# Forming the Strassen right operands in place and on VectorE, three single-pair chunk pairs at either end, and weight roundings on ScalarE

## The chip, the cores and the metric

The kernel runs on one core of a Trainium2 chip. The metric is the time of one execution in device microseconds (us), as the median of three runs. The page and the rows come from one further execution that the hardware profiler recorded. PE is TensorE, DVE is VectorE, ACT is ScalarE, POOL is GpSimd; SP issues nearly all DMAs.

## The reference

One encoder layer runs over two requests (16 meta tokens and 256 prompt tokens; 16 meta tokens and 1024 sample tokens) with shared float32 weights:

```python
h = concat([meta, x])
h = h + 0.5 * swiglu(rmsnorm(h, norm_ffn1), ffn1_w_gate, ffn1_w_up, ffn1_w_down)
u = rmsnorm(h, norm_mix) @ w_in
o = diff_attention(q, k, v, lam, bias)      # 4 heads, two softmax maps each
p = pool_mixer(p_in, pool_w, pool_scale)    # windows 2, 4, 8, 16
h = h + concat([rmsnorm(o) * 0.8, p]) @ w_out
h = h + 0.5 * swiglu(rmsnorm(h, norm_ffn2), ffn2_w_gate, ffn2_w_up, ffn2_w_down)
y = rmsnorm(h, norm_final)[:, 16:]
# swiglu(x, g, u, d) = (silu(x @ g) * (x @ u)) @ d ; D_MODEL 1024, D_FF 2816
```

## The kernel before

Activations stand transposed: features on the 128 partitions (8 k-tiles `c`), tokens along the row, 1296 tokens in FFN1 (the two requests' shared meta tokens doubled), 1280 in FFN2. A float32 matmul is done as three matmuls of rounded parts (`mm3`, L157 to L159): high weight by high input, low by high, high by low. Forming a part therefore takes two steps: a rounding ("hi") and a subtraction of it ("lo"). For weights POOL makes the hi (L145) and DVE the lo (L148); for inputs ACT makes the hi (L142).

**Gate and up projections.** Each FFN splits its tokens into four blocks (324 or 320 tokens) that go in two pairs, (0,2) and (1,3). For each of 11 chunk pairs `j` of 256 output features, `gate_up` calls `seven` once for the gate weight and once for the up weight. `seven` computes a 2x2 block product (two halves of the features of the input by two blocks of tokens, two output chunks) by seven products in place of eight, in the order b11, t1, t2, b22, t3, b21, t4. A product is 4 k-tiles by 3 matmuls for each pair in `subs`; a `seven` is 84 matmuls on one pair and 168 on both. Its left operands come from `s_parts`: four raw quarter blocks, and four sums of them that DVE forms (L359, L362, L367, L374). It has three raw buffers of 512 KB (`wraw`), and five of the parts' buffers (RING). Results are kept by ACT (L399) and added by DVE (L409, L413, L417); up's results go to memory (L439) and are read again as `hraw` by the down projection, where ACT rounds them and DVE or POOL makes the lo.

**Right operands T.** For a token pair, `t_tasks` makes b11, b22, b21, t1 to t4: DVE multiplies by gain and by the row of inverse norms (L322) into an `xf` buffer, POOL makes four subtractions, ACT the hi and DVE the lo, k-tile pair `c` by pair (`c` 0 to 3). All seven products need all four `c`. Pair 0's T is formed from `h` while tokens of the second group come in (`token_in`, `token_rows`); then `h` goes to `h1_d`, and pair 1's T is formed from there, as tasks that `pump()` starts after each k-tile of a product.

**Order of chunk pairs.** Chunk pair 0 runs for pair 0 alone while T[1] is formed ("first single set"); chunk pairs 1 to 10 run on both pairs; chunk pair 0 runs for pair 1 alone ("second single set"), after which the freed memory takes `h` again (three whole loads, L634) for the down projection. FFN2 does the same; its `h` comes out of the w_out projection (L1182), which also runs pair by pair with the same (0,2), (1,3), forms T[0] when the first pair is done, and adds up squares for the norms (L1145, L1154).

Within an engine the order is what the tile scheduler chose; a DMA waits on SP for its operands with the DMAs behind it.

Of the kernel before, what the change touches and what calls it, by code (L numbers as in the profile page):

```python
# [19 lines left out]
P = 128  # L20
# [17 lines left out]
PAIRS = ((0, 2), (1, 3))  # L38
# [60 lines left out]
def encoder(ctx: ExitStack, tc: tile.TileContext, a: dict):  # L99
# [207 lines left out]
    def t_tasks(key, T, n, get, gain, rows, xp):  # L307
# [3 lines left out]
        def load(c):  # L311
            for cc in (c, c + 4):
                for side in range(2):
                    x[cc, side] = get(cc, side)

        def norm(c):
            for cc in (c, c + 4):
                for side in range(2):
                    src, dst = x[cc, side]
                    if dst is None:  # L320
                        dst = xp.tile([P, NS], F32, tag="xf", name="xf", bufs=5)[:, :n]
                    nc.vector.scalar_tensor_tensor(  # L322
                        out=dst, in0=src, scalar=gain[:, cc : cc + 1], in1=rows[side], op0=ALU.mult, op1=ALU.mult
                    )
                    x[cc, side] = dst

        def sums(c):
            b11, b12, b21, b22 = (x.pop((cc, side)) for cc in (c, c + 4) for side in range(2))
            split(c, b11=b11, b22=b22, b21=b21)
# [16 lines left out]
        return out

    def s_parts(w, j, tp):

        r0, r1 = raw_cols(w, 2 * j), raw_cols(w, 2 * j + 1)  # L350
# [14 lines left out]
        hi_pool(h2, f2)  # L365
# [4 lines left out]
        hi_pool(h4, f4)  # L370
# [52 lines left out]
    def gate_up(j, T, blocks, subs, wg, wu, hid, tp, bufs):  # L423

        n = blocks[0][1]
# [9 lines left out]
        def up(s, fi, ti, c, in_psum=False):  # L435
            o = g[s, fi, ti] if in_psum else c
            nc.vector.tensor_mul(o, g[s, fi, ti], c)
            t0 = blocks[PAIRS[s][ti]][0]
            nc.sync.dma_start(out=hid[2 * j + fi][:, t0 : t0 + n], in_=o)  # L439

        seven(wg, j, T, n, subs, tp, temp, gate)
# [4 lines left out]
    def down_tasks(h, blocks, hid, wd, hp):  # L446
        order = list(range(1, NF // 2)) + [0]
# [89 lines left out]
    def token_in(i, tok, h, ss):  # L537

        t0, m = TOK[i]
        for half in range(2):  # L540
# [5 lines left out]
            (nc.vector.tensor_copy if half else nc.scalar.copy)(out=h[:, 4 * half : 4 * half + 4, t0 : t0 + m], in_=psv)  # L546
        nc.scalar.activation(out=tok, in_=tok, func=AF.Square, accum_out=ss[:m])
# [45 lines left out]
    tasks.extend(
        t_tasks(
            ("t", 0),
            T[0],
            NS,
            lambda c, side: (h[:, c, part_of(PAIRS[0][side])], None),
            gains["norm_ffn1"],
            [row[:, part_of(b)] for b in PAIRS[0]],  # L600
            xp,
        )
    )
# [4 lines left out]
    token_rows(TOK_ORDER[1], ss[1], row)
    for lo, hi in ((0, 384), (384, 640), (640, 1024), (1024, T1)):
        nc.sync.dma_start(out=h1_d[:, :, lo:hi], in_=h[:, :, lo:hi])  # L610
    pump(len(tasks))
# [12 lines left out]
    for j in range(1, NF // 2):  # L624
        gate_up(j, T, BS1, (0, 1), wg, wu, hid1_d, tp, 18)
# [6 lines left out]
    first, down = down_tasks(h, BL1, hid1_d, a["ffn1_w_down"][0], hp)  # L632
    for b, (s, n) in enumerate(BL1):
# [698 lines left out]
```

## Time and profile before

| | |
|---|---|
| median of 3 runs | 2537.6 us (2537.16 to 2540.35) |
| the profiled execution | 2537.2 us, span 2535.4 us |
| mean granted PE clock | 0.959 of full |
| busy PE, DVE, ACT, POOL | 2354.2, 1484.1, 597.5, 675.7 us |
| PE's share of the chain that ended last | 81% |

A busy PE is not a PE at its peak: its matmuls take longer when the granted clock is low, and the gaps between them are small. The stages along the time are FFN1 to about 650 us with its down projection behind, w_in and the attention up to 1469, w_out to 1617, FFN2's gate and up to 2205, down projection and last norm to the end.

### The profile page before, as it was taken

To read this page: it belongs to the slowest core of one execution; us is meant where nothing else is said; L and a number is where in the kernel's file an instruction comes from. 1 tells how busy PE (TensorE), PEld (TensorE's weight loads), DVE (VectorE), ACT (ScalarE), POOL (GpSimd) and SP (SyncE) were. 2 spreads that over 40 slices of the span, in tenths; PEclk is the share of its full clock that TensorE was granted. 3 is DMA by queue.
4 is the path that set the end of the run, shared out by engine and by line. 5 is a ranking of instruction groups with operands and counts; after the bars stand their busy time and mean duration, and the time that the engine had idled before them with its cause. 6 is when DMAs were issued, how large, how long until landed. Compare 5 with 4: busy or idle time off the path is not lost.

```text
span 2535.4 us, 38469 instructions
## 1 busy us (share of the span) xinstructions
PE 2354.2 (93%) x14578; PEld 2202.0 (87%) x14578; DVE 1484.1 (59%) x2726; ACT 597.5 (24%) x1341; POOL 675.7 (27%) x879
## 2 busy tenths in 40 slices
PE   3799999999999998999878887799999999999998
PEld 3699999999888887899778887689999999888886
DVE  6844544544767766344477737575444454666765
ACT  5321111111111113111467623221111111111113
POOL 3411111111212124111377635331111111211112
PEclk6899999999999999999999998789999999999999
DMA  6312221224422323645644154322212222622322
GB/s 206 90 55 74 73 71 57 78 76 147 132 76 85 96 71 113 174 147 165 165 132 122 48 155 127 104 78 77 77 55 76 72 70 64 222 83 77 98 71 84
DMA packets 270386, 256.30 MB, mean 101 GB/s; under 512 B 20369, under 2 KB 229865, under 8 KB 269689
## 3 DMA queue, kind: packets, MB, share of 16 engines
q1 hardware_dynamic: 270200, 253.85, 32.8%
q8 instruction: 115, 1.88, 0.3%
q14 instruction: 71, 0.57, 0.1%
HBM read 182.40 MB, written 75.61 MB: 102 GB/s over the span
## 4 chain that ended last, share of the span: by engine, by line
PE 81%; DVE 5%; POOL 4%; DMA 4%; issue 2%; ACT 2%; SPq 1%; POOLq 0%; ACTq 0%; DVEq 0%
PE bank L157 26%; PE bank L158 26%; PE bank L159 26%; DMA v<-v_d 1%; DVE xf L322 1%; DVE wl L148 1%; POOL l L831 1%; PE bank L848 1%; PE pair L800 1%; PE pair L801 1%; DMA hc<-h_d 1%; POOL xf L330 1%; DMA hraw<-hid_d 1%; PE bank L237 1%; SPq L783 0%
## 5 line engine op out<-in xcount | busy, mean ns | idle before, releaser
L145 POOL TENSOR_SCALAR wh<-wraw 128x512 fp32r<-128x512 f32 x296 | 213.2, 723 | 788.0 <-PE bank L159 490.4
L148 DVE TENSOR_TENSOR wl<-wraw,wh 128x512 fp32r<-128x512 f32 x296 | 226.6, 769 | 329.4 <-POOL wh L145 328.8
L479 DVE SCALAR_TENSOR_TENSOR h<-bank,h 128x272 f32<-128x272 f32 (+2 forms) x528 | 312.7, 601 | 151.3 <-PE bank L159 147.1
L157 PE MATMUL bank<-hl,wh 128*128 128x512 f32 (+2 forms) x1056 | 380.1, 360 | 0.0
L158 PE MATMUL bank<-hl,wl 128*128 128x512 f32 (+2 forms) x1056 | 379.4, 359 | 0.0
L159 PE MATMUL bank<-hl,wh 128*128 128x512 f32 (+2 forms) x1056 | 378.8, 359 | 0.0
L399 ACT COPY hid<-bank 128x324 f32<-128x324 f32 (+1 forms) x264 | 112.9, 428 | 659.5 <-PE bank L159 650.5
L145 POOL TENSOR_SCALAR wh<-ws 128x512 fp32r<-128x512 f32 x192 | 126.2, 660 | 526.7 <-PE bank L159 327.0
L159 PEld LDWEIGHTS bank<-hl,wh 128*128 128x128 f32 x1056 | 199.1, 189 | 31.8
L157 PEld LDWEIGHTS bank<-hl,wh 128*128 128x128 f32 x1056 | 199.1, 189 | 31.7
L158 PEld LDWEIGHTS bank<-hl,wl 128*128 128x128 f32 x1056 | 198.9, 188 | 31.5
L148 DVE TENSOR_TENSOR wl<-ws,wh 128x512 fp32r<-128x512 f32 x192 | 142.2, 744 | 99.5 <-POOL wh L145 99.5
L142 ACT CAST hl<-hraw 128x272 fp32r<-128x272 f32 (+2 forms) x132 | 72.5, 552 | 519.3 <-PE bank L158 395.2
L157 PE MATMUL bank<-t2h,wh 128*128 128x324 f32 (+1 forms) x352 | 112.1, 318 | 13.0 <-POOL wh L145 13.0
L157 PE MATMUL bank<-t1h,wh 128*128 128x324 f32 (+1 forms) x352 | 110.9, 316 | 7.0 <-POOL wh L145 7.0
L157 PE MATMUL bank<-b22h,wh 128*128 128x324 f32 (+1 forms) x352 | 110.7, 314 | 7.2 <-POOL wh L145 5.0
L158 PE MATMUL bank<-t4h,wl 128*128 128x324 f32 (+1 forms) x352 | 110.1, 313 | 6.5 <-DVE wl L148 6.5
L158 PE MATMUL bank<-t2h,wl 128*128 128x324 f32 (+1 forms) x352 | 111.6, 317 | 4.6 <-DVE wl L148 4.6
L157 PE MATMUL bank<-t3h,wh 128*128 128x324 f32 (+1 forms) x352 | 110.1, 313 | 4.7 <-POOL wh L145 4.7
L157 PE MATMUL bank<-t4h,wh 128*128 128x324 f32 (+1 forms) x352 | 110.0, 312 | 3.5 <-DVE hid L413 3.5
L158 PE MATMUL bank<-t1h,wl 128*128 128x324 f32 (+1 forms) x352 | 111.7, 317 | 1.2 <-DVE wl L148 0.7
L158 PE MATMUL bank<-t3h,wl 128*128 128x324 f32 (+1 forms) x352 | 110.3, 313 | 1.6 <-DVE wl L148 1.6
(217 smaller groups left out, 6293.8 us busy)
## 6 DMA issues: line engine op xcount, KB each, us to landing
wraw<-in_ffn_w_gate SPq DMA_DIRECT2D x48, 512.0 KB
wraw<-in_ffn_w_up SPq DMA_DIRECT2D x48, 512.0 KB
hraw<-hid_d SPq DMA_DIRECT2D x88, 256.0 KB
wraw<-in_ffn_w_down SPq DMA_DIRECT2D x44, 512.0 KB
hid_d<-hid SPq DMA_DIRECT2D x88, 162.0 KB
hid_d<-hid SPq DMA_DIRECT2D x88, 160.0 KB
k<-k_d SPq DMA_DIRECT2D x32, 260.0 KB
h<-h_d SPq DMA_DIRECT2D x4, 2048.0 KB
```

The lines of the kernel that those rows point to most:

```text
L142: nc.scalar.copy(out=out, in_=in_)
L145: nc.gpsimd.tensor_scalar(out=out, in0=in_, scalar1=1.0, scalar2=1.0, op0=ALU.mult, op1=ALU.mult)
L148: nc.vector.tensor_sub(out, in_, hi.bitcast(F32))
L157: nc.tensor.matmul(out=ps, lhsT=wh, rhs=xh, start=first, stop=False, skip_group_check=on)
L158: nc.tensor.matmul(out=ps, lhsT=wl, rhs=xh, start=False, stop=False, skip_group_check=on)
L159: nc.tensor.matmul(out=ps, lhsT=wh, rhs=xl, start=False, stop=last, skip_group_check=on)
L237: nc.tensor.matmul(out=ps[:, j * m : (j + 1) * m], lhsT=r[:, j : j + 1].broadcast_to([m, P]), rhs=ident[:m, :m], start=True, stop=True,)
L322: nc.vector.scalar_tensor_tensor(out=dst, in0=src, scalar=gain[:, cc : cc + 1], in1=rows[side], op0=ALU.mult, op1=ALU.mult)
L330: nc.gpsimd.tensor_sub(b11, b12, b11)
L399: nc.scalar.copy(out=to[s], in_=ps[s])
L479: nc.vector.scalar_tensor_tensor(out=h[b][:, m], in0=ps, scalar=0.5, in1=h[b][:, m], op0=ALU.mult, op1=ALU.add)
L800: nc.tensor.matmul(out=ps[:, m], lhsT=qs, rhs=kh[:, ks], start=True, stop=False)
```

## The change

- Pair 0's T is formed **in place** in `h`, in product order: fourteen steps (`t_in_place`), each of two k-tiles; all sums are on DVE, and lo's are 128x648. Since `h` is overwritten, each token tile goes to `h1_d` right after it came in (eleven writes in place of four), and the norm waits for these. The first two raw weights are loaded ahead of it.
- Pair 1's T (`t_loaded`) has its loads, norms, lo's, sums and lo's as separate tasks with gaps between them; sums on DVE.
- Chunk pairs 0, 1, 2 run for pair 0 alone, 3 to 10 for both, 0, 1, 2 for pair 1 alone, in both FFNs (`SINGLE1`, `SINGLE2`). Weight parts of a chunk pair that runs alone are loaded and formed twice.
- The hi of weight parts in `s_parts` is on ACT; of the other weights it stays on POOL.
- `h` for the down projection is loaded in 12 pieces, one for each seven calls of `pump`.
- FFN2's pairs are (0,1), (2,3). `cat` has a tile for each block and channel; four channels of block 1 are loaded during the attention. `hc` loads run two ahead. T[0] is formed in place under w_out's second pair; gate_up starts when it is done, and the second pair's norm rows are made inside gate_up.

```diff
-PAIRS = ((0, 2), (1, 3))
+PAIRS1 = ((0, 2), (1, 3))
+PAIRS2 = ((0, 1), (2, 3))
+SINGLE1 = 3
+SINGLE2 = 3
...
-    def parts_of(raw):
+    def parts_of(raw, hi_of=hi_pool):
...
-        hi_pool(wh, raw)
+        hi_of(wh, raw)
...
+    def t_split(T, c, k, **f):
+        for name, v in f.items():
+            th, tl = (t[:, c : c + k] for t in T[name])
+            hi_act(th, v)
+            lo_dve(tl, v, th)
+
+    def spread(key, fs, gap):
+        return [(key, g) for f in fs for g in [f] + [None] * gap]
...
+        def t1(c):
+            x = X(c, 0)
+            nc.vector.tensor_sub(x, norm(c, 1), x)
+            t_split(T, c, 2, t1=x)
...
+        return [lambda f=f, c=c: f(c) for f in (b11, t1, t2, b22, t3, b21, t4) for c in (0, 2)]
...
-            nc.gpsimd.tensor_sub(b11, b12, b11)
-            nc.gpsimd.tensor_sub(b12, b22, b12)
-            nc.gpsimd.tensor_sub(b22, b22, b11)
-            nc.gpsimd.tensor_sub(b21, b21, b22)
...
+            nc.vector.tensor_sub(b11, b12, b11)
+            nc.vector.tensor_sub(b12, b22, b12)
+            nc.vector.tensor_sub(b22, b22, b11)
+            nc.vector.tensor_sub(b21, b21, b22)
...
-        hi_pool(h1, f1)
+        hi_act(h1, f1)
...
+        nc.sync.dma_start(out=h1_d[:, :, t0 : t0 + m], in_=h[:, :, t0 : t0 + m])
         nc.scalar.activation(out=tok, in_=tok, func=AF.Square, accum_out=ss[:m])
...
+    tasks.extend(spread(("t", 1), [None, lambda: token_rows(TOK_ORDER[1], ss[1], row), None], 4))
+    tasks.extend(spread(("t", 1), t_loaded(T[1], NS, h1_d, places[1], gains["norm_ffn1"], rows[1], xp), 5))
+    for j in range(SINGLE1):
+        gate_up(j, T, places, NS, (0,), wg, wu, hid1_d, tp, 9, raws if j == 0 else None)
...
-    for b, (s, n) in enumerate(BL1):
-        nc.sync.dma_start(out=h[b], in_=h1_d[:, :, s : s + n])
-    first = first()
-    gate_up(0, T, BS1, (1,), wg, wu, hid1_d, tp, 10)
...
+    tasks.extend(spread(("h", 0), load_h(h, h1_d, BL1), 6))
+    for j in range(SINGLE1):
+        if j == SINGLE1 - 1:
+            parts0 = first()
+        gate_up(j, T, places, NS, (1,), wg, wu, hid1_d, tp, 10)
...
-                        hc = tx.tile([P, NS], F32, tag="hc", name="hc", bufs=2)[:, :n]
-                        nc.sync.dma_start(out=hc, in_=h_d[:, m, s : s + n])
...
+                        hc = got[b, m]
...
-    ensure(("row", PAIRS[1][1]))
-    pump(len(tasks))
+    ensure(("t", 0))
```

The next two fences are DVE at the start of FFN1, first of before and then of after: T[0] being formed beside the token tiles of the second group (`h` copies from a `bank`); b11l to t4l are the lo parts of T, `xf` and `h` their unrounded values.

```order
L148 TENSOR_TENSOR t2l<-xf,t2h 128x324
L148 TENSOR_TENSOR t4l<-xf,t4h 128x324
L322 SCALAR_TENSOR_TENSOR xf<-h,g_norm_ffn_208,row 128x324 x4
L546 COPY h<-bank 128x4x128
L148 TENSOR_TENSOR b11l<-xf,b11h 128x324
L148 TENSOR_TENSOR b22l<-xf,b22h 128x324
L148 TENSOR_TENSOR b21l<-xf,b21h 128x324
```

```order
L152 TENSOR_TENSOR t1l<-h,t1h 128x648
L589 COPY h<-bank 128x4x128
L338 TENSOR_TENSOR h<-h 128x2x324
L328 SCALAR_TENSOR_TENSOR h<-h,g_norm_ffn_208,row 128x324
L589 COPY h<-bank 128x4x128
L343 TENSOR_TENSOR h<-h 128x2x324
L152 TENSOR_TENSOR t1l<-h,t1h 128x648
```

Before, the last lo of one k-tile (t4l) stands ahead of the first of the next (b11l), so no product is whole until all is; after, one operand follows another, whole, and the subtractions stand among them on DVE.

The next two are SP where the both-pair chunk pairs of FFN1 end and the second single set begins, before and after: `h` is the residual, `hraw` the hidden values for the down projection, `wraw` the raw weights.

```order
L634 DMA h_5864<-h_d 128x8x272
L439 DMA hid_d_104<-hid 128x324 x2
L634 DMA h_5865<-h_d 128x8x512
L634 DMA h_5866<-h_d 128x8x512
L454 DMA hraw<-hid_d_85 128x272
L454 DMA hraw<-hid_d_86 128x272
L454 DMA hraw<-hid_d_85 128x512
L164 DMA wraw<-in_ffn_w_up 128x8x128
```

```order
L670 DMA h_5411<-h_d 128x2x512
L670 DMA h_5409<-h_d 128x2x272
L670 DMA h_5410<-h_d 128x2x512
L168 DMA wraw<-in_ffn_w_up 128x8x128
L168 DMA wraw<-in_ffn_w_gate 128x8x128
L670 DMA h_5411<-h_d 128x2x512
L670 DMA h_5409<-h_d 128x2x272
L670 DMA h_5410<-h_d 128x2x512
L670 DMA h_5411<-h_d 128x2x512
L505 DMA hraw<-hid_d_89 128x272
```

Eight of the twelve pieces of `h` still stand ahead of up's second raw weight, but no `hraw` does.

The last two are ACT in the both-pair chunk pairs (gate, then up), before and after: COPY L399 and L451 keep a product's sum, `wh` is the hi of a weight part.

```order
L399 COPY hid_2944<-bank_2918 128x324 [waits DMAHW2_49,PE_49]
L399 COPY hid_2946<-bank_2931 128x324 [waits DMAHW3_49,PE_49]
L399 COPY hid_2984<-bank_2958 128x324 [waits DMAHW4_49,PE_49]
L399 COPY hid_2986<-bank_2971 128x324 [waits DMAHW5_49,PE_49]
L399 COPY hid_3018<-bank_2918 128x324 [waits DVE_49,PE_49,Activation_49]
```

```order
L451 COPY hid_3261<-bank_3235 128x324 [waits DMAHW7_49,PE_49]
L451 COPY hid_3263<-bank_3248 128x324 [waits DMAHW0_49,PE_49]
L146 CAST wh_3403<-wraw_3189 128x512 [waits DMAHW5_49,Activation_49]
L451 COPY hid_3295<-bank_3195 128x324 [waits PE_49]
L451 COPY hid_3297<-bank_3208 128x324 [waits PE_49]
L146 CAST wh_3439<-wraw_3435 128x512 [waits DMAHW6_49,Activation_49]
```

Weight roundings now stand behind copies that wait for PE.

## Rows read from the trace of the kernel before

**Rows 1.** Windows: length, busy (x count) of PE, PEld, DVE, ACT, POOL, PEclk, DMA share, GB/s.

```profile
0.00:20.00 20.00, 9.25 (x53) 8.81 (x54) 5.15 (x15) 10.82 (x19) 2.03 (x7) 0.94 0.92 311
80.00:100.00 20.00, 8.13 (x36) 7.14 (x36) 17.85 (x31) 9.21 (x21) 10.46 (x10) 0.74 0.27 83
120.00:600.00 480.00, 480.00 (x3234) 480.00 (x3233) 231.79 (x401) 87.43 (x197) 84.02 (x135) 1.00 0.22 70
...
1620.00:1640.00 20.00, 9.04 (x32) 7.57 (x30) 16.68 (x27) 7.60 (x19) 10.35 (x11) 0.50 0.14 41
...
1680.00:2160.00 480.00, 480.00 (x3273) 480.00 (x3272) 235.45 (x407) 87.78 (x199) 86.99 (x138) 1.00 0.22 70
```

**Rows 2.** Timeline of PE: start, length, idle before and what ended it.

```profile
61.67 0.64 PE L157 MATMUL bank<-b11h,wh 128*128 128x324 f32 x1
...
112.36 0.31 PE L157 MATMUL bank<-b11h,wh 128*128 128x324 f32 x1
...
611.42 0.31 PE L157 MATMUL bank<-b11h,wh 128*128 128x324 f32 x1
...
650.09 0.29 PE L157 MATMUL bank<-hl,wh 128*128 128x272 f32 x1
...
1477.55 0.64 PE L157 MATMUL bank<-ch,wh 128*128 128x320 f32 x1 [8.23 <-ACT ch L142]
...
1573.62 0.64 PE L158 MATMUL bank<-ch,wl 128*128 128x320 f32 x1 [11.07 <-DVE wl L148]
...
1616.19 1.23 PE L1154 MATMUL bank<-ones,acc 128*80 128x1 f32 x8 [5.51 <-DVE acc L1145]
1617.27 0.61 PE L157 MATMUL bank<-b11h,wh 128*128 128x320 f32 x1
...
1676.34 0.31 PE L157 MATMUL bank<-b11h,wh 128*128 128x320 f32 x1
...
2169.45 0.31 PE L157 MATMUL bank<-b11h,wh 128*128 128x320 f32 x1
...
2205.34 0.28 PE L157 MATMUL bank<-hl,wh 128*128 128x256 f32 x1
```

**Rows 3.** Timeline of DVE while T[0] and the first weight parts are formed.

```profile
21.28 0.56 DVE L322 SCALAR_TENSOR_TENSOR xf<-h,g_norm_ffn,row 128x324 f32<-128x324 f32 x1 [2.44 <-ACT row L562]
...
34.16 1.17 DVE L148 TENSOR_TENSOR b21l<-xf,b21h 128x324 fp32r<-128x324 f32 x1
...
40.02 0.49 DVE L148 TENSOR_TENSOR b11l<-xf,b11h 128x324 fp32r<-128x324 f32 x1
40.42 0.49 DVE L148 TENSOR_TENSOR b21l<-xf,b21h 128x324 fp32r<-128x324 f32 x1
...
58.93 0.68 DVE L148 TENSOR_TENSOR wl<-ws,wh 128x512 fp32r<-128x512 f32 x1
59.53 0.68 DVE L367 TENSOR_TENSOR ws<-wraw,ws 128x512 f32<-128x512 f32 x1
```

**Rows 4.** The page's groups: busy us and mean ns of one, then idle time before.

```profile
L145 POOL TENSOR_SCALAR wh<-wraw 128x512 fp32r<-128x512 f32 x296 | 213.2, 723 | 788.0 <-PE bank L159 490.4
L148 DVE TENSOR_TENSOR wl<-wraw,wh 128x512 fp32r<-128x512 f32 x296 | 226.6, 769 | 329.4 <-POOL wh L145 328.8
...
L399 ACT COPY hid<-bank 128x324 f32<-128x324 f32 (+1 forms) x264 | 112.9, 428 | 659.5 <-PE bank L159 650.5
...
L142 ACT CAST hl<-hraw 128x272 fp32r<-128x272 f32 (+2 forms) x132 | 72.5, 552 | 519.3 <-PE bank L158 395.2
```

**Rows 5.** Timeline of SP, and of DVE, in FFN1's second single set.

```profile
624.53 0.38 SPq L164 DMA_DIRECT2D wraw<-in_ffn_w_up  x1
...
634.09 0.68 DVE L359 TENSOR_TENSOR ws<-wraw 128x512 f32<-128x512 f32 x1
```

More of the change, by code (lines that the diff above doesn't have):

```diff
@@ L305, in t_tiles, with t_in_place, norm, b11 @@
         return {k: tuple(pool_.tile([P, 4, n], F32R, tag=f"{k}{t}", name=f"{k}{t}", bufs=1) for t in "hl") for k in T_NAMES}
-    def t_tasks(key, T, n, get, gain, rows, xp):
+    def t_split(T, c, k, **f):
[5 more added lines that the diff above has]
+        return [(key, g) for f in fs for g in [f] + [None] * gap]
+    def t_in_place(T, X, gain, rows):
+        def norm(c, side):
+            x = X(c, side)
+            for i in range(2):
+                nc.vector.scalar_tensor_tensor(
+                    out=x[:, i], in0=x[:, i], scalar=gain[:, c + i : c + i + 1], in1=rows[side], op0=ALU.mult, op1=ALU.mult
+                )
+            return x
+        def b11(c):
+            t_split(T, c, 2, b11=norm(c, 0))
+        def t1(c):
+            x = X(c, 0)
+            nc.vector.tensor_sub(x, norm(c, 1), x)
+            t_split(T, c, 2, t1=x)
+        def t2(c):
+            x = X(c, 0)
+            nc.vector.tensor_sub(x, norm(c + 4, 1), x)
+            t_split(T, c, 2, t2=x)
+        def b22(c):
+            t_split(T, c, 2, b22=X(c + 4, 1))
+        def t3(c):
+            x = X(c, 1)
+            nc.vector.tensor_sub(x, X(c + 4, 1), x)
+            t_split(T, c, 2, t3=x)
+        def b21(c):
+            t_split(T, c, 2, b21=norm(c + 4, 0))
+        def t4(c):
+            x = X(c + 4, 0)
+            nc.vector.tensor_sub(x, x, X(c, 0))
+            t_split(T, c, 2, t4=x)
+        return [lambda f=f, c=c: f(c) for f in (b11, t1, t2, b22, t3, b21, t4) for c in (0, 2)]
+    def t_loaded(T, n, src, starts, gain, rows, xp):
         x = {}
@@ L437, in up, with down_tasks @@
             nc.vector.tensor_mul(o, g[s, fi, ti], c)
-            t0 = blocks[PAIRS[s][ti]][0]
+            t0 = places[s][ti]
             nc.sync.dma_start(out=hid[2 * j + fi][:, t0 : t0 + n], in_=o)
-        seven(wg, j, T, n, subs, tp, temp, gate)
+        seven(wg, j, T, n, subs, tp, temp, gate, raws)
         seven(wu, j, T, n, subs, tp, temp, up)
-    def down_tasks(h, blocks, hid, wd, hp):
-        order = list(range(1, NF // 2)) + [0]
+    def down_tasks(h, blocks, hid, wd, hp, single):
+        order = list(range(single, NF // 2)) + list(range(single))
         def prep(g):
@@ L583, in encoder @@
         nc.vector.memset(t, 1.0)
-    def part_of(b):
-        return slice(BS1[b][0], BS1[b][0] + NS)
+    places = [[BS1[b][0] for b in pair] for pair in PAIRS1]
+    rows = [[row[:, s : s + NS] for s in pair] for pair in places]
     toks = [token_dma(i, hp) for i in TOK_ORDER[0]]
     load_gain("norm_ffn1")
+    raws = raw_cols(wg, 0), raw_cols(wg, 1)
     for j, i in enumerate(TOK_ORDER[0]):
@@ L592, in encoder @@
     token_rows(TOK_ORDER[0], ss[0], row)
[L593 to L603, printed above, removed]
+    steps_ = t_in_place(T[0], lambda c, side: h[:, c : c + 2, places[0][side] : places[0][side] + NS], gains["norm_ffn1"], rows[0])
+    for f in steps_[:2]:
+        f()
     for j, i in enumerate(TOK_ORDER[1]):
-        pump(2)
         token_in(i, token_dma(i, hp), h, ss[1][:, j : j + 1])
-    pump(len(tasks))
[L608 to L611, printed above, removed]
+        for f in steps_[2 + 3 * j : 5 + 3 * j]:
+            f()
     gst.close()
@@ L623, in encoder @@
     bst_, tp = scope("tmpb", side="right")
-    for j in range(1, NF // 2):
-        gate_up(j, T, BS1, (0, 1), wg, wu, hid1_d, tp, 18)
+    for j in range(SINGLE1, NF // 2):
+        gate_up(j, T, places, NS, (0, 1), wg, wu, hid1_d, tp, 18)
     bst_.close()
@@ L1162, in encoder @@
     raws = [raw_cols(w_out, m) for m in range(2)]
-    for b in PAIRS[0]:
+    places = [[BS2[b][0] for b in pair] for pair in PAIRS2]
+    for b in PAIRS2[0]:
         s = BS2[b][0]
@@ L1166, in encoder, with load_hc @@
         nc.sync.dma_start(out=h[b], in_=h_d[:, :, s : s + n])
-    for i, pair in enumerate(PAIRS):
-        for b in pair:
-            if b:
-                for c in order:
-                    cat_part(b, c, tx, 4)
+    for b in range(3):
+        for c in CAT_ORDER:
+            if (b, c) not in cat:
+                cat_part(b, c, tx, 3)
+    ahead = [(b, m) for m0 in range(0, KC, 2) for b in PAIRS2[1] for m in (m0, m0 + 1)]
+    got = {}
+    def load_hc():
+        if ahead:
+            b, m = ahead.pop(0)
+            got[b, m] = tx.tile([P, NS], F32, tag="hc", name="hc", bufs=3)[:, :n]
+            nc.sync.dma_start(out=got[b, m], in_=h_d[:, m, BS2[b][0] : BS2[b][0] + n])
+    for i, pair in enumerate(PAIRS2):
+        if i:
+            load_hc()
+            load_hc()
+            for c in CAT_ORDER:
+                cat_part(pair[1], c, tx, 3)
         for m0 in range(0, KC, 2):
```

142 lines of the change are left out of this document (70 added, 72 removed).

## The prediction, made before the changed kernel ran

> **What bounds the kernel now.** I read the windows first [rows 1], for the granted clock and PE's share by stage, then PE's timeline at the stages' edges [rows 2], then what DVE does there [rows 3, 5], and took durations from the page's groups and from spacings [rows 3, 4]. In the both-pair stages of the two FFNs PE is full: 3234 matmuls in 480 us at clock 1.00 (0.1484 us each), 3273 in FFN2 (0.1467) [rows 1]. There DVE is busy 232 of 480 us and ACT 87: no other engine is near its end. What is not full are four places beside these: the first single set of each FFN, w_out, and the second single sets. In them PE waits for DVE or for a weight part, and the clock falls to 0.50 to 0.74 [rows 1]; at 0.50 (1.2 GHz) 32 matmuls took 9.04 us, 0.28 each. A single set is 168 matmuls: 24.9 us (FFN1), 24.6 us (FFN2) at full clock. Measured [rows 2]:
>
> - FFN1's first product starts at 61.67; the set ends at 112.36.
> - Its second set, 611.42 to 650.09, takes 38.7, 13.7 too many.
> - w_out: PE begins to wait at 1469.3 (1477.55 less 8.23) and starts FFN2 at 1617.27, 148.0. The loops issue 768 matmuls, of which 48 had run; 720 are worth 105.6; 42.4 too many.
> - FFN2's first set, to 1676.34, takes 59.1, 34.4 too many.
> - Its second set, 2169.45 to 2205.34, takes 35.9, 11.2 too many.
>
> FFN2 thus loses 88.0 us around its edges, FFN1 13.7 and its slow start. The change goes at these.
>
> **FFN1's start.** DVE sets it. Undisturbed, a 128x324 takes 0.41 us from one to the next, a 128x512 0.60 [rows 3]. Before, DVE can start normalizing at 21.28 [rows 3], but T is whole only at 61. After, the norm also waits until the first group's six `h1_d` writes (3.1 MB) landed. The nearest row is the first window: 311 GB/s with the engines 92% busy [rows 1]; at that rate 3.1 MB last 10 us, most of it beside the copies that feed it, so I take 24. From there the changed order gives DVE, for T[0], 16 norms at 0.45, 8 subtractions and 14 lo's of two k-tiles at 0.82, and five copies at 0.6: 28 us. T[1] is 60 instructions at 0.41, 24.6. A `seven` needs 11 weight instructions at 0.60 and 3 (gate) or 7 (up) on 128x324: 7.8 or 9.5. By the order DVE stands at the end of T[1] when it has done the weights of four and a half sevens, some of those ahead of 24: 86 us of work, to 110. Ten products (120 matmuls, 17.8) are then left to PE: 128 without any wait. For waits on token tiles, the round trip through ACT and stretches at half clock I add 2 to 9 and take 133. Six sevens are over then. Before, two were over at 112.36 and four more would be worth 49.9, to 162.3. **Gain 29 (25 to 35).** T[1]'s own cost is nothing only while the three sets' 74.8 us of PE cover it; DVE has 52 + 24.6 us in the same span, so the cover is thin and the set goes at DVE's pace, which the sum has in it.
>
> The extra forming costs loads too: eight more sevens' weights, 8 MB, in a kernel that moves 70 GB/s in these stages [rows 1]: hidden.
>
> **FFN1's second sets.** Before, up's second raw weight was issued at 624.53 behind `h` and `hraw`, and DVE began its first sum at 634.09 [rows 5]. After, `hraw` comes only ahead of the third set, when 50 us of singles have passed; but eight of the twelve `h` pieces still stand ahead of that weight, and gate's first sum still stands on DVE behind the last results of the both-pair stage. I leave one such restart: 4 (1 to 8) in place of 13.7. **Gain 10 (6 to 13).**
>
> **FFN2's start.** Five losses take the place of 88.0.
> - The wait for `cat` (8.23) stays, since the `h` loads still stand ahead of it: 8, and 1.5 for the clock after it.
> - Under w_out's second pair, T[0], with the weights' and sums' own work between, is 26 us of DVE by the same count beside 28 of PE. The 11.07 us for one `wl` [rows 2] came from a whole T standing ahead of it on DVE; now weight lo's stand between the steps. One still stands behind the eighth sum: 6 (2 to 12).
> - The 5.51 for `acc` [rows 2] goes, but the second pair's norm columns now stand on DVE ahead of gate's first sum, behind the last projection: 7.
> - The three single sets: DVE has 53.8 us up to the last T[1] lo (counted from the changed order, at the same spacings), against 44 of PE by then; with restarts 14 (9 to 20).
> - The second sets, as in FFN1: 3 (1 to 7).
>
> Sum 39.5, **gain 48 (36 to 58)**.
>
> **Hi on ACT.** In a both-pair `seven` ACT gets seven roundings more. Its rows are 0.43 for a 128x324 copy and 0.55 for a rounding of mixed shapes [rows 4], so some 4 us in 24.9, on an engine that was busy 87 of 480 us. Its queue is in order, and roundings stand behind copies that wait for PE. With five buffers a part is due four products after its buffer comes free, 14 us; copy, rounding and lo are 1.6. I take zero, and price the contrary below. DVE gains by POOL's silence: beside POOL's subtractions a b21 lo took 1.17, alone 0.49 [rows 3], and the mean `wl` was 0.77 [rows 4]. The sum already goes by undisturbed spacings. The Trainium skill, GPSIMD Engine Reference, section Specifications, says that POOL shares its SBUF interfaces with DVE and contends with DVE instructions that have two SBUF inputs; these rows agree. Had POOL stayed busy, six sevens would have 42 `wl` at 0.77 in place of 0.60, 7 us more for each first set.
>
> **The attention** keeps its order but for three more `cat` loads: 0, within 5 either way. The sum: 29 + 10 + 48 = 87. The profiled execution took 2537.2 (span 2535.4 and 1.8 around it), beside a median of 2537.6. 2537.2 less 87 is 2450.
>
> **The rivals.**
>
> *The single sets are bound elsewhere.* Twelve sevens run alone in each FFN; each needs two raw loads through three buffers, ACT, DVE and PE in turn within 12.5 us. If restarts and the half clock cost 1.5 to 3 us more in each of 24, the gain falls by 36 to 72: 2486 to 2515. For: every single set now loses 11 to 34 us, and one fall to 0.50 makes 84 matmuls take 23.5 us. Against: these sets formed T or loaded `h` and `hraw` within two sevens, and six now share that.
>
> *The writes hold the start.* Eleven `h1_d` writes of 128-token rows stand on SP ahead of the second group's tokens, and the norm waits for six of them. If they move at half the 311 GB/s, the start is 10 us later: 2460. The DMA share of 0.92 in that window [rows 1] speaks for it; that the second window's tokens come in while DVE has T to form speaks against. The Trainium skill, DMA: Bandwidth & Descriptors, section Measured, gives 341 GB/s for 1 MB and 138 for 64 KB and asks for 1 MiB transfers; the change cuts `h1_d` and `h` the other way. By its lower figure, an estimate, the six writes would last 23 us and the time be 2462; the row's 311 was reached with pieces of 512 KB, so I hold the upper end likelier.
>
> *More comes back.* If the singles are not bound by DVE but keep PE full, FFN2's start loses 22 rather than 39.5 and FFN1 starts 6 earlier: 2427.
>
> *ACT's queue holds the both-pair stages (slower).* 32 both-pair sevens now get their hi from ACT. If the copies of a product and the roundings behind them lock step, each of three such roundings delays its part by rounding and lo, 1.15: 3.5 us in each, 110 in all, 2560. It decides from 2.7 us a `seven` (87/32). Against it stand the four products of lead.
>
> *It does not do what it says.* If the scheduler puts the in-place steps behind the waits that they were to avoid (h1_d writes after all tokens, the last `acc`), the start and FFN2's edge stay and only the eased loads of the second sets remain, 10, paid by the extra forming: 2537 within 5.
>
> **How the numbers follow.** Forecast 2450 with its own range 2430 to 2478 (the ends of its three gains, not all at once; the writes' rival lies in it): 0.64. Singles bound elsewhere, 2478 to 2515: 0.20. More comes back, below 2430: 0.06. No change: 0.04. Slower: 0.06. To hold 8 in 10, the range takes the forecast's own, the better half of the first rival and a little below: 2428 to 2492. Faster by over 0.2% (5 us, about what a measurement of this kernel can tell from no change): 0.64 + 0.20 + 0.06 = 0.90; within: 0.04; slower: 0.06.
>
> **What would show it.** FFN1's first products near 30 us and its third single set over near 133; both-pair stages still at 1.00 without PE waits, at 24.9 and 24.6 us a `seven`; the second sets' six sevens near 79 us; no 11 us wait for `wl` in w_out; FFN2's first product 10 to 15 us after the last projection's matmuls at most, and three sets in 88. Wrong would be: PE waiting for `wh` by ACT in the both-pair stages, a clock at 0.50 through a single set, a first norm after 30, or singles waiting for raw loads.

## The result and the profile after

| | before | after |
|---|---|---|
| median | 2537.4 us (4 runs, 2534.7 to 2540.35) | 2452.1 us (4 runs, 2450.31 to 2457.24) |
| ratio | | 0.9667, 95% interval 0.9649 to 0.9685 |
| the profiled execution, its span | 2537.2, 2535.4 | 2450.3, 2448.5 |
| mean granted clock | 0.959 | 0.979 |
| busy PE, DVE, ACT, POOL | 2354, 1484, 598, 676 | 2336, 1506, 804, 388 |

PE's timeline of the changed kernel at the same edges as [rows 2]: start, length, and the idle time before with what ended it.

```profile
34.70 0.42 PE L161 MATMUL bank<-b11h,wh 128*128 128x324 f32 x1
...
134.47 0.31 PE L161 MATMUL bank<-b11h,wh 128*128 128x324 f32 x1
...
533.69 0.31 PE L161 MATMUL bank<-b11h,wh 128*128 128x324 f32 x1
...
612.34 0.28 PE L161 MATMUL bank<-hl,wh 128*128 128x272 f32 x1
...
1520.83 0.63 PE L162 MATMUL bank<-ch,wl 128*128 128x320 f32 x1 [6.11 <-DVE wl L152]
...
1549.95 0.31 PE L163 MATMUL bank<-cl,wh 128*128 128x320 f32 x1
1550.10 0.31 PE L161 MATMUL bank<-b11h,wh 128*128 128x320 f32 x1
...
1556.88 0.63 PE L161 MATMUL bank<-t1h,wh 128*128 128x320 f32 x1 [3.78 <-ACT wh L146]
...
1646.34 0.31 PE L161 MATMUL bank<-b11h,wh 128*128 128x320 f32 x1
...
2040.82 0.31 PE L161 MATMUL bank<-b11h,wh 128*128 128x320 f32 x1
...
2118.36 0.28 PE L161 MATMUL bank<-hl,wh 128*128 128x256 f32 x1
```

The first single set of FFN1 ends at 134.47, the second runs from 533.69 to 612.34; FFN2's first product is at 1550.10, its sets run to 1646.34 and from 2040.82 to 2118.36. A single set now has six sevens where it had two; to compare, four sevens are added to the old sets at full clock (49.9 us in FFN1, 49.3 in FFN2), as the prediction did. The row of w_out is taken from the last matmul of the attention (1464.36 and 1421.83 in PE's timelines).

| stage | before | after | gain | forecast |
|---|---|---|---|---|
| FFN1 to the end of the first sets | 162.3 | 134.5 | 27.8 | 29 |
| FFN1 second sets | 88.6 | 78.7 | 9.9 | 10 |
| down, w_in, attention | 814.3 | 809.5 | 4.8 | 0 |
| w_out, to FFN2's first product | 152.9 | 128.3 | 24.6 | } 40 |
| FFN2 first sets | 108.4 | 96.2 | 12.1 | } |
| FFN2 second sets | 85.2 | 77.5 | 7.7 | 8 |
| sum, with the rest equal (330.1 behind FFN2's sets in both) | | | 86.9 | 87 |

The windows of after, columns as in [rows 1]:

```profile
40.00:60.00 20.00, 13.78 (x61) 13.06 (x62) 15.59 (x32) 12.06 (x26) 1.17 (x1) 0.74 0.67 185
60.00:80.00 20.00, 17.58 (x108) 15.85 (x106) 19.57 (x41) 10.53 (x23) 0.00 (x0) 1.00 0.41 119
80.00:100.00 20.00, 18.92 (x118) 17.68 (x119) 19.84 (x42) 12.99 (x28) 0.00 (x0) 1.00 0.34 95
100.00:120.00 20.00, 18.74 (x115) 16.95 (x114) 19.44 (x41) 11.03 (x23) 0.00 (x0) 1.00 0.35 105
...
160.00:520.00 360.00, 360.00 (x2426) 360.00 (x2425) 173.61 (x297) 120.00 (x249) 0.00 (x0) 1.00 0.22 70
...
1480.00:1500.00 20.00, 18.69 (x118) 18.41 (x118) 13.55 (x34) 5.60 (x10) 5.91 (x6) 0.83 0.49 163
1500.00:1520.00 20.00, 14.72 (x101) 14.46 (x99) 20.00 (x30) 7.15 (x12) 7.52 (x7) 0.93 0.32 102
...
1580.00:1600.00 20.00, 15.56 (x88) 14.18 (x87) 18.19 (x39) 9.37 (x22) 0.00 (x0) 0.91 0.39 118
...
1680.00:2020.00 340.00, 340.00 (x2319) 340.00 (x2318) 169.44 (x292) 113.17 (x234) 0.00 (x0) 1.00 0.22 70
```

In FFN1's first sets DVE is busy for 19.4 to 19.8 of 20 us from 60 to 120 us, with PE at clock 1.00 and POOL at 0; from 40 to 60 us it still has room (15.6). The both-pair stages are full as before; there ACT is now busy for a third of the time (120 of 360 us), and a seven takes 24.95 us (399.2 for sixteen) as before (499.1 for twenty, from 112.36 to 611.42). ACT's queue holds nothing up there.

DVE's timeline of after at the start, to set beside [rows 3], and the last lo of T[1]:

```profile
22.55 1.42 DVE L152 TENSOR_TENSOR wl<-ws,wh 128x512 fp32r<-128x512 f32 x2
23.89 1.95 DVE L328 SCALAR_TENSOR_TENSOR h<-h,g_norm_ffn,row 128x324 f32<-128x324 f32 x4
25.75 0.83 DVE L152 TENSOR_TENSOR b11l<-h,b11h 128x648 fp32r<-128x648 f32 x1
...
116.72 0.49 DVE L152 TENSOR_TENSOR t4l<-xf,t4h 128x324 fp32r<-128x324 f32 x1
```

The first norm starts at 23.89 with no idle time ahead of it: DVE comes straight from the weight lo's.

### The profile page after: what moved, and what is told of

It reads as the page before. It is cut to its first block, busy times and chain, and to the rows that moved or that the text cites. A ratio compares the mean times of both kernels' runs of the same rounds, so it can differ in the third digit from the quotient of the medians.

```text
span 2448.5 us, 38316 instructions
## 1 busy us (share of the span) xinstructions
PE 2336.4 (95%) x14578; PEld 2181.6 (89%) x14578; DVE 1506.1 (62%) x2834; ACT 803.8 (33%) x1705; POOL 387.6 (16%) x479
## 4 chain that ended last, share of the span: by engine, by line
PE 82%; DVE 8%; DMA 4%; POOL 2%; issue 2%; ACT 1%; SPq 1%; POOLq 0%; ACTq 0%; DVEq 0%
PE bank L162 26%; PE bank L161 26%; PE bank L163 26%; DVE wl L152 1%; DMA v<-v_d 1%; PE bank L893 1%; PE pair L845 1%; PE pair L846 1%; PE bank L242 1%; DMA wraw<-in_ffn_w_up 1%; DMA wraw<-in_ffn_w_gate 1%; DMA cat<-cat_d 1%; POOL l L876 0%; POOL ry L223 0%; DVE h L328 0%
## 5 line engine op out<-in xcount | busy, mean ns | idle before, releaser
L152 DVE TENSOR_TENSOR wl<-wraw,wh 128x512 fp32r<-128x512 f32 x320 | 235.3, 740 | 296.1 <-ACT wh L146 219.8
L155 POOL TENSOR_TENSOR hl<-hraw,hl 128x272 fp32r<-128x272 f32 (+1 forms) x44 | 34.7, 790 | 1239.9 <-ACT hl L146 1148.9
L146 ACT CAST wh<-ws 128x512 fp32r<-128x512 f32 x224 | 138.4, 620 | 252.4 <-PE bank L163 156.0
L451 ACT COPY hid<-bank 128x324 f32<-128x324 f32 (+1 forms) x264 | 112.7, 427 | 279.5 <-PE bank L163 278.9
L152 DVE TENSOR_TENSOR wl<-ws,wh 128x512 fp32r<-128x512 f32 x224 | 153.7, 689 | 73.2 <-ACT wh L146 72.4
L149 POOL TENSOR_SCALAR wh<-wraw 128x512 fp32r<-128x512 f32 x152 | 115.1, 759 | 526.4 <-PE bank L163 245.2
L161 PE MATMUL bank<-b21h,wh 128*128 128x324 f32 (+1 forms) x352 | 110.4, 314 | 0.3
```

Source lines behind the costliest of these rows:

```text
L146: nc.scalar.copy(out=out, in_=in_)
L149: nc.gpsimd.tensor_scalar(out=out, in0=in_, scalar1=1.0, scalar2=1.0, op0=ALU.mult, op1=ALU.mult)
L152: nc.vector.tensor_sub(out, in_, hi.bitcast(F32))
L155: nc.gpsimd.tensor_sub(out, in_, hi.bitcast(F32))
L161: nc.tensor.matmul(out=ps, lhsT=wh, rhs=xh, start=first, stop=False, skip_group_check=on)
L451: nc.scalar.copy(out=to[s], in_=ps[s])
```

## The experiments

Most undo or alter one part of the changed kernel; one adds a part to the kernel before, and the last four widen gaps and sets, some of them together. A table by stages stands at the end of the section.

**Hi of the weights on POOL again.**

```diff
-        hi_act(h1, f1)
+        hi_pool(h1, f1)
# and so for the other six parts of s_parts
```

> The changed kernel with one part undone: the hi of the gate and up weight parts is on POOL again. Theory (the first single sets go at DVE's pace, and POOL's work beside DVE slows DVE): the weight lo's of the first sets go from 0.60 us back towards 0.77, about 7 us more in each FFN's first set, both-pair stages unchanged: about 2466. Rival (roundings behind ACT's copies cost something in the both-pair stages): those stages get shorter than 24.95 us a seven and the time is 2450 or less.

Measured: 2499.0 us, ratio to before 0.9855 (0.9839 to 0.9872), 46.8 more than the changed kernel. The both-pair stages did not move (399.25), so the rival falls; but the theory had put 14 us where there were 47, and it had put them in the first sets alone. The second sets, where no T is formed, pay as much: 10.9 and 12.8. Groups in FFN1's second set by line, tiles and shape: busy us and mean ns, idle before. First with the hi on POOL:

```profile
L152 DVE TENSOR_TENSOR wl<-ws,wh 128x512 fp32r<-128x512 f32 x24 | 21.3, 900 | 3.6 <-POOL wh L149 3.4
L149 POOL TENSOR_SCALAR wh<-ws 128x512 fp32r<-128x512 f32 x24 | 18.4, 772 | 51.4 <-DVE ws L411 30.7 <-DVE ws L419 9.7 <-DVE ws L426 7.4
L149 POOL TENSOR_SCALAR wh<-wraw 128x512 fp32r<-128x512 f32 x21 | 17.7, 850 | 11.5 <-PE bank L163 5.3 <-DVE hid L488 2.3 <-POOL wh L149 1.7
```

and the changed kernel:

```profile
L152 DVE TENSOR_TENSOR wl<-ws,wh 128x512 fp32r<-128x512 f32 x24 | 16.3, 688 | 2.7 <-ACT wh L146 2.5
L146 ACT CAST wh<-ws 128x512 fp32r<-128x512 f32 x24 | 14.8, 620 | 17.1 <-DVE ws L411 11.1 <-DVE ws L419 4.7 <-DVE ws L426 0.6
L146 ACT CAST wh<-wraw 128x512 fp32r<-128x512 f32 x17 | 10.5, 622 | 0.0
```

Each part takes 0.15 to 0.23 us more for its hi and 0.21 more for its lo, and both lie on the chain from raw weight to PE. Seven parts at some 0.4 are 2.8 us a seven; six sevens 17, of which 11 to 13 come out. PE's waits for a hi in this second set (total us, times, longest), first with the hi on POOL, then of the changed kernel:

```profile
PE bank L161 <- POOL wh L149: 6.0, 4, 3.3
```

```profile
PE bank L161 <- ACT wh L146: 1.0, 1, 1.0
```

The first sets of FFN1 and of FFN2 as one window each, columns as in [rows 1], with the hi on POOL and then of the changed kernel:

```profile
35.30:147.30 112.00, 89.95 (x517) 82.04 (x517) 101.98 (x180) 39.14 (x85) 34.97 (x39) 0.94 0.41 118
1575.40:1682.50 107.10, 88.06 (x539) 83.05 (x538) 92.98 (x167) 27.43 (x62) 36.71 (x44) 0.92 0.33 101
```

```profile
34.70:134.50 99.80, 87.03 (x517) 80.90 (x516) 90.25 (x178) 57.86 (x121) 1.17 (x1) 0.95 0.47 131
1550.10:1646.30 96.20, 84.62 (x538) 80.95 (x537) 81.89 (x167) 49.81 (x104) 1.99 (x2) 0.95 0.37 112
```

There DVE's own busy time grows by 11.7 and 11.1 us, for nearly the same work, where the sets lose 12.8 and 10.8: where DVE sets the pace, its longer instructions are of the size of the whole loss.

**Three single chunk pairs added to the kernel before, nothing else.**

```diff
-    gate_up(0, T, BS1, (0,), wg, wu, hid1_d, tp, 10)
+    for j in range(3):
+        gate_up(j, T, BS1, (0,), wg, wu, hid1_d, tp, 10)
# and so for the second sets, for FFN2, and the order of the down projection
```

> The kernel before with three chunk pairs in each single set and nothing else of the change. Theory (the first sets are held by how T is formed, the sets alone only help the second sets): second sets gain 10 and 8, first sets within 5: about 2518. Rival (the number of sets carries most of the gain): 2490 or below.

Measured: 2565.4 us, ratio 1.0119 (1.0104 to 1.0134): slower than before by 30, where the theory had a gain of 18. It fell where it thought single sevens free. With the hi on POOL four more of them cost 6.1 and 5.5 us in FFN1's two sets and 8.9 and 7.6 in FFN2's, beyond their 49.9 and 49.3. Its windows behind the first two sevens:

```profile
132.00:152.00 20.00, 19.23 (x130) 19.00 (x129) 14.34 (x24) 2.12 (x6) 6.49 (x10) 1.00 0.46 139
152.00:168.00 16.00, 14.52 (x98) 14.29 (x97) 11.02 (x18) 2.97 (x7) 4.58 (x7) 1.00 0.30 87
```

PE is not full, though the last lo of T[1] stood at 99.5 us and DVE is at 70%. PE's waits in these windows end with DVE's addition of results (0.8 us) and with a POOL hi (1.5). In FFN1's second set, where no T is formed, most of them end with a POOL hi:

```profile
PE bank L157 <- POOL wh L145: 10.1, 4, 5.0
```

So with the hi on POOL more single sevens cost time in the kernel before; in the changed kernel they gain (next experiment). That the engine of the hi alone makes this difference is not shown, since the rest of the change is missing here too.

**One chunk pair in each single set.**

```diff
-SINGLE1 = 3
-SINGLE2 = 3
+SINGLE1 = 1
+SINGLE2 = 1
```

> The changed kernel with one chunk pair in each single set instead of three. Theory (three sets are needed to cover T[1] on DVE and to spread the loads of h and of the hidden values): FFN1's first set ends about 10 us later than the same work does now, FFN2's about 3, and the second sets lose some 10 us each again instead of 4: about 2480. Rival (the gain came from the order in which T is formed and from the roundings, the number of sets does not matter): 2452 to 2458.

Measured: 2469.1 us, ratio 0.974 (0.9725 to 0.9754), 17 more than the changed kernel and 11 less than expected. The first sets cost 5.7 and 2.7 more (10 and 3 were expected; they are counted to the end of a wait of 14.3 and 13.5 us for a weight lo, which stands in the first both-pair seven), the both-pair stages 2.2 and 1.8, the second sets only 2.0 and 3.3. So hidden values and dealt-out loads within one chunk pair cost little. The old second sets are not made again by this: by SP's timeline six of the twelve pieces of `h` here stand behind up's second raw weight, and before all three whole loads stood ahead of it.

**The residual in three whole loads.**

```diff
-            nc.sync.dma_start(out=h[b][:, c : c + 2], in_=src[:, c : c + 2, s : s + n])
+            nc.sync.dma_start(out=h[b], in_=src[:, :, s : s + n])   # for the three blocks, at once
```

> The changed kernel with the residual loaded again in three whole loads at the start of the second single sets. Theory (the loss of the old second sets came from h and hidden values that were loaded and rounded within one chunk pair; now only h stands there): 2 to 4 us more in each second set, about 2458. Rival 1 (the dealing out is what eased the second sets): 8 to 10 us more in each, about 2470. Rival 2 (the pieces bring nothing, eight of twelve stood ahead of up's weight anyway): 2452.

Measured: 2463.0 us, ratio 0.9719 (0.9705 to 0.9734), 11 more. The second sets lose 6.0 and 8.3 more, together nearer to the first rival (16 to 20) than to the theory (4 to 8). Dealing out the loads is worth more than I gave it, though eight of the twelve pieces stand ahead of up's second weight.

**FFN2's pairs as before.**

```diff
-PAIRS2 = ((0, 1), (2, 3))
+PAIRS2 = ((0, 2), (1, 3))
...
-    for b in range(3):
+    for b in (0, 2, 1):
```

> The changed kernel with FFN2's and w_out's pairs (0,2), (1,3) as before; block 2's eight channels are then loaded ahead of block 1's other four. Theory (the 8 us wait for the attention's output at the start of w_out went because block 1 has four channels at hand while the rest comes in): the wait returns with 5 to 9 us, 1 to 2 more for the clock behind it: about 2460. Rival (it went because of the order of loads, whatever the blocks): 2452.

Measured: 2459.3 us, ratio 0.9702 (0.9687 to 0.9716), 7 more. PE's timeline of it:

```profile
1435.56 0.63 PE L161 MATMUL bank<-ch,wh 128*128 128x320 f32 x1 [8.40 <-ACT ch L146]
```

The wait is back with its old size (8.23 in [rows 2]); in the changed kernel it is gone. It is the choice of blocks, with the loads in their order, that covers it.

**Lo of T[1] done twice.**

```diff
             t_split(T, c, 1, **f)
+            for k, v in f.items():
+                th, tl = (t[:, c : c + 1] for t in T[k])
+                lo_dve(tl, v, th)
```

> The changed kernel with the 28 lo subtractions of each second pair's T done twice on DVE (the same values). Theory (DVE sets the pace of both first single sets): 28 x 0.41 = 11.5 us more in each FFN, less what slack DVE has there: FFN1 9 to 11, FFN2 6 to 11, about 2470. Rival (PE, or the chain from ACT to DVE to PE, sets it, and DVE has room): 2452 to 2457.

Measured: 2479.2 us, ratio 0.9781 (0.9765 to 0.9797), 27 more: 12.5 in FFN1's first sets and 16.2 in FFN2's for 11.5 us of added work in each. DVE has no room there. In FFN2 more is lost than was added. A window of its first set, and PE's longest waits in the whole set, first of this kernel, then of the changed one:

```profile
1621.00:1641.00 20.00, 11.94 (x74) 10.64 (x72) 19.66 (x45) 8.94 (x20) 0.00 (x0) 1.00 0.24 70
```

```profile
PE bank L161 <- ACT wh L146: 11.9, 4, 4.3
PE bank L162 <- DVE wl L152: 10.0, 8, 2.6
```

```profile
PE bank L161 <- ACT wh L146: 7.4, 4, 3.8
PE bank L162 <- DVE wl L152: 4.1, 8, 1.0
```

In the window PE is busy 60% of the time at a full clock, and in the 20 us before the clock is 0.83. The waits for weight parts grow by 10.4 us. That the added work does this because it stands bunched, with gaps of 3 between T[1]'s steps, ahead of the weight lo's is argued here; the wider gaps below bear it out.

**Two lo's of each first-set seven on POOL.**

```diff
-        lo_dve(wl, raw, wh)
+        lo_of(wl, raw, wh)      # lo_pool for parts a12 and a22 where subs is (0,)
```

> The changed kernel with the lo of the last two weight parts of each seven of the first single sets on POOL instead of DVE: DVE is relieved of 12 x 0.60 = 7 us a set. Theory (POOL and DVE slow each other where both read two tensors): what DVE saves is about lost again on its neighbours, 2447 to 2457. Rival (DVE's pace alone counts, POOL's work is free): 7 us less in each FFN, about 2440.

Measured: 2457.7 us, ratio 0.9695 (0.968 to 0.9709), 5.6 more: the first sets lose 3.6 and 5.4 although DVE has 7 us less to do in each. Groups in FFN2's first set, of this kernel (two lines) and of the changed one (one):

```profile
L155 POOL TENSOR_TENSOR wl<-wraw,wh 128x512 fp32r<-128x512 f32 x12 | 17.0, 1432 | 73.7 <-ACT wh L146 73.7
L152 DVE TENSOR_TENSOR wl<-wraw,wh 128x512 fp32r<-128x512 f32 x6 | 6.3, 1056 | 5.4 <-ACT wh L146 5.4
```

```profile
L152 DVE TENSOR_TENSOR wl<-wraw,wh 128x512 fp32r<-128x512 f32 x18 | 12.0, 688 | 1.8 <-ACT wh L146 1.8
```

A lo takes 1.43 us on POOL for 0.69 on DVE, and DVE's own lo of the raw part that stays goes to 1.06. DVE's busy time in the set, 81.9 us in the changed kernel, is still 80.8: nearly all that was taken off it comes back in longer instructions. Handing POOL work that reads two tensors was no relief.

**T[0] by k-tiles in place of by products.**

```diff
-        return [lambda f=f, c=c: f(c) for f in (b11, t1, t2, b22, t3, b21, t4) for c in (0, 2)]
+        return [lambda f=f, c=c: f(c) for c in (0, 2) for f in (b11, t1, t2, b22, t3, b21, t4)]
```

> The changed kernel with the fourteen steps of the first pair's T in another order: all seven operands for k-tiles 0 and 1, then all for 2 and 3, instead of one operand after the other. The work is the same. Theory (FFN1's first set is set by DVE's total work, so that an early first product is worth little): first product some 10 us later, third set over 0 to 4 later, about 2454. Rival (the order by products is what gained): 10 or more later, 2462 or above.

Measured: 2448.5 us, ratio to before 0.9656 (0.9641 to 0.967); the changed kernel's 0.9667 lies in that interval. The first set ends 0.5 later. The first product did not move by the 10 us that I expected (35.24 against 34.70), since a product begins with its first two k-tiles. The product order, which the first point of the change names, is worth nothing that these runs can tell.

**T[1] spread over the whole set, then four chunk pairs, then T[0] spread wider.**

```diff
-t_loaded(T[1], NS, h1_d, ...), 5))          # FFN1; FFN2: 3
+t_loaded(T[1], NS, h1_d, ...), 6))          # FFN2: 7
```

> The changed kernel with the second pair's T spread over nearly the whole of the three single chunk pairs: gaps of 6 in place of 5 between its steps in FFN1, of 7 in place of 3 in FFN2 (168 calls of pump; the steps then take 155 and 160). Theory (in the first sets DVE has 12.4 less 8.65 = 3.8 us to spare in a seven, T[1] needs 24.6 in all; bunched into half of the set, in FFN2, it holds PE back there and leaves DVE idle behind): FFN2's first set loses 12 to 16 us in place of 22, FFN1's 0 to 3 less: about 2443. Rival (the loss is the start and its chain, not where T[1] stands): 2450 to 2454.

```diff
-SINGLE1 = 3
+SINGLE1 = 4                                 # SINGLE2 too; both gaps 9
```

> The changed kernel with four chunk pairs in each single set and gaps of 9 in both FFNs, so that T[1] is spread over eight sevens. Theory (as for the gaps, and FFN1's first set too is held by T[1] on DVE): each first set loses 8 to 14 us less than now, each second set 1 to 2 more for the seven that is added: about 2436. Rival (single sevens cost more than their 12.4 us whatever stands beside them): each added chunk pair costs 1 to 3 us in each set, 2454 or above.

```diff
-                tasks.extendleft(reversed(spread(("t", 0), steps_, 3)))
+                tasks.extendleft(reversed(spread(("t", 0), steps_, 5)))   # with the gaps 6 and 7
```

> As with the gaps of 6 and 7, and T[0]'s steps under w_out's second pair with gaps of 5 in place of 3. Theory (the 6 us wait for one weight lo in w_out comes from T[0]'s steps that stand ahead of it on DVE): 4 to 7 us less than with the gaps alone. Rival (that lo waits for its place among the buffers or for POOL): as with the gaps alone, or longer, since T[0] ends later: 0 to 6 more.

Measured: 2442.4 (ratio 0.9637, 0.9624 to 0.965), 2432.9 (0.9602, 0.9589 to 0.9615) and 2438.2 (0.9622, 0.9609 to 0.9635). The gaps take 9.0 us from FFN2's first sets, within the 6 to 10 expected; FFN1 gains nothing: its first sets end 2.0 us earlier, but T[1] now ends later (its last lo at 123.7 us for 116.7), and the first both-pair seven takes 3.9 us longer. With four chunk pairs that wait is gone, and FFN1's second set ends 7.2 us earlier than in the changed kernel, with the added work taken out. The first sets gain 7.7 and 11.9 us (8 to 14 were expected), the second sets pay 0.5 and 3.1 (1 to 2). A window of each FFN's first sets with four:

```profile
100.00:120.00 20.00, 20.00 (x136) 20.00 (x135) 19.69 (x40) 12.65 (x27) 0.00 (x0) 1.00 0.44 135
...
1583.00:1603.00 20.00, 20.00 (x138) 20.00 (x137) 19.08 (x39) 12.29 (x27) 0.00 (x0) 1.00 0.51 155
```

PE and DVE are full together. The wider gaps of T[0] take 5.1 us from w_out: PE's waits there, first with the gaps of 6 and 7 alone, then with T[0]'s too (total us, times, longest):

```profile
PE bank L162 <- DVE wl L152: 6.3, 2, 6.1
```

```profile
PE bank L162 <- DVE wl L152: 1.1, 3, 0.6
```

So that lo did wait behind T[0]'s steps.

**Four chunk pairs and the wider T[0] together.**

> Four chunk pairs in each single set with gaps of 9, and T[0]'s steps under w_out with gaps of 5. Theory (the two gains are in different stages): both add, 4 us less than with the four sets and gaps alone, about 2429. Rival (T[0]'s later end takes from FFN2's first set what w_out gives): 2433.

Measured: 2427.8 us, ratio to before 0.9582 (0.9568 to 0.9595), 5 less than with the four chunk pairs and gaps alone, whose interval overlaps this one a little; in the profiled executions 4.3 us of it lie ahead of FFN2's first product, where they were expected. Both add, and this is the fastest of all.

The profiled spans by stage, against the changed kernel's (the last row against the kernel before). Where the number of sevens in a set differs, it is made equal at full clock:

| kernel | FFN1 first | FFN1 second | to FFN2's first product | FFN2 first | FFN2 second | span |
|---|---|---|---|---|---|---|
| hi on POOL | +12.8 | +10.9 | +1.5 | +10.8 | +12.8 | +48.9 |
| one chunk pair | +5.7 | +2.0 | +0.5 | +2.7 | +3.3 | +18.1 |
| h whole | +0.3 | +6.0 | -1.4 | -0.9 | +8.3 | +12.3 |
| pairs (0,2) | +0.5 | -0.3 | +10.3 | -1.6 | -0.3 | +8.6 |
| lo of T[1] twice | +12.5 | -0.2 | -1.0 | +16.2 | +0.9 | +28.4 |
| two lo's on POOL | +3.6 | +0.5 | -2.6 | +5.4 | +0.2 | +8.4 |
| T[0] by k-tiles | +0.5 | -0.6 | -0.4 | -1.2 | -0.2 | -1.9 |
| gaps of 6 and 7 | -2.0 | -0.3 | -0.3 | -11.5 | -0.3 | -8.1 |
| gaps of 6 and 7, T[0] wider | -3.0 | +0.2 | -5.5 | -10.7 | +0.4 | -13.8 |
| four chunk pairs, gaps of 9 | -7.7 | +0.5 | +0.2 | -11.9 | +3.1 | -15.3 |
| four chunk pairs, gaps of 9, T[0] wider | -8.8 | +0.7 | -4.1 | -12.0 | +3.3 | -20.2 |
| three sets in the kernel before | +6.1 | +5.5 | -1.1 | +8.9 | +7.6 | +27.0 |

(The both-pair stages make up most of the rest: 2.2 and 1.8 us for one chunk pair, 0.6 each for the two lo's on POOL, 3.9 and 2.5 for the gaps of 6 and 7, 1.8 and 3.0 for these with T[0] wider.)

## Why the prediction was right, and where it was right for the wrong reason

**The sum held, and most of its terms.** 2450 was forecast, 2452.1 measured. FFN1's start (27.8 for 29), both second sets (9.9 for 10, 7.7 for 8) and FFN2's start with w_out (36.7 for 40) came near what was worked out; the attention, with the down projection and w_in, gave 4.8, within the 5 that was left open; no run shows what gave it.

**DVE sets FFN1's first sets: shown.** The norm started at 23.89 (24). The last lo of T[1] stood at 116.72 (110), and the third set ended at 134.47 (133), 17.75 later, with 114 matmuls and one wait of 0.3 us in between; the forecast had 120 matmuls in 17.8. DVE was busy for 98% of the time from 60 to 120 us, and 11.5 us of DVE work more moved the end by 12.5. The reason for the 24 was off: DVE was still busy with the weight lo's when the norm began, so the writes of `h1_d` were not the last to be waited for. The rival of the writes (2460) didn't come; that the order by products gives nothing fits the same picture.

**Hi on ACT: the price that was wrong, and the largest part.** The prediction took zero for what ACT's roundings cost the both-pair stages, and that held. For POOL's, had they stayed, it had 7 us for each first set and nothing for the second sets. With POOL it is 12.8, 10.9, 10.8 and 12.8: 47 us, more than half of what the change brings. The sum held all the same, since it went by spacings of DVE that POOL doesn't disturb. The row that it rested on, a mean `wl` of 0.77 in [rows 4], is a mean over the whole kernel, most of it from stages where PE hides it, and a length that was set against a spacing of 0.60 (alone the length is 0.68, [rows 3]); in a single set the lo took 0.90, and the hi, whose 0.62 on ACT against 0.77 to 0.85 on POOL I had not compared at all, lies on the same chain. And I looked for its price only where T is formed.

**The second sets: the right size for another reason.** I put their 13.7 and 11.2 down to loads of `h` and `hraw` within one chunk pair. The loads are part of it (whole loads cost 6.0 and 8.3 again), but with one chunk pair, the loads dealt out and all else changed the sets lose only 2.0 and 3.3, and with three and the hi on POOL they lose 10.9 and 12.8. The kernel before with three sets and nothing else shows that room alone is not it: more of it for the loads, and 5.5 and 7.6 worse. The parts are not additive: in spans, undoing four of them one at a time costs 48.9 + 18.1 + 12.3 + 8.6 = 87.9, about the whole gain, but by stages they do not fit it: 19.3 for 27.8 in FFN1's first sets, 18.6 and 24.1 for 9.9 and 7.7 in the second sets. Writing T in place and DVE's sums were not undone.

**FFN2's start: the sum near, in part by luck, its terms off against each other.** The wait for `cat` that I left at 8, with 1.5 for the clock after it, went to zero through the new pairs, as the kernel with the old pairs shows (8.40). The 6 under w_out's second pair were 6.11. Yet w_out lost 18.4 us where 15.5 were forecast: from the attention's last matmul it takes 128.3 for 110 us of matmuls (749 at 0.1467). Beside the 6.11 there are smaller waits, 2.5 in all, and a clock of 0.83 to 0.93 in its second half, which the forecast had at nothing. The norm columns were to cost 7 ahead of FFN2's first product; that product starts 0.15 us behind w_out's last matmul. The three sets were to lose 14 and lost 22.3 (96.2 less six sevens at 12.3), of which a wider spread of T[1] gave 9.0 back.

**Rivals.** That ACT's queue holds the both-pair stages is excluded (24.95 us a seven in both kernels). That singles are bound elsewhere didn't come, but the run with POOL shows that it was close: 48.9 us more by one engine's choice. (The upper end of that rival is a slip: 72 us from 2450 is 2522, not 2515.) That more comes back had the right mechanism, singles at PE's pace, and it needed a spread of T[1] that the change doesn't have; with it, with four chunk pairs and T[0] spread wider, another kernel, 2427.8 was measured where that rival had 2427.

What stays open: how the 47 us of the roundings split between POOL's longer hi and DVE's longer instructions, since no run changed one without the other (in the first sets DVE's busy time alone is of the size of the loss, in the second sets PE waits for the hi); and what writing T in place and DVE's sums are worth by themselves.

## What to carry to other kernels

A mean over the whole trace hides what an instruction costs where it is on the path: take the duration from the stage, and for every link of the chain. Where one engine is full in a stage, doubling a piece of its work shows it in one run. Spreading the same work over the time in which that engine has room gave 9.0 us in FFN2's first sets here; the one other order of it that was tried gave nothing clear. An engine that looks idle is no free help if it slows the one that is full.

## What the runs showed of the hardware

A rounding of a 128x512 weight part, which reads one tensor, took 0.62 us on ACT and as much on POOL where DVE was idle (184 of them in the kernel before; the other 304, beside DVE, took 0.75 on average). In FFN1's second set it took 0.77 to 0.85 on POOL, and DVE's subtractions of two tensors went from 0.69 to 0.90. A subtraction of two tensors took 1.43 us on POOL beside DVE and brought DVE's of the raw part that stayed to 1.06. The Trainium skill, GPSIMD Engine Reference, section Specifications, has contention for DVE instructions with two SBUF inputs, and these rows agree.

In w_out the granted clock was 0.83 in a window in which PE was busy for 18.7 of 20 us (1480 to 1500). By PE's timeline short matmuls of one and of 80 columns and one wait of 1.3 us stood ahead of the fall; from 1486.6 to 1493.3 a 128x320 matmul then took 0.27 us from one to the next, the half clock (1.2 GHz), and 0.15 before and behind.
